# State-space loop of a decoder trunk: output tables summed on TensorE, input tables first, sine tables and one Toeplitz transfer moved

## Chip, cores and metric

The kernel runs on one core of one Trainium2 chip. The metric is the device time of one execution in microseconds (us). The kernel before has a median of 1282.83 us over 3 runs, from 1282.32 to 1284.73.

## What is computed

The reference is a decoder trunk for one sequence of 512 tokens with 16 learned tokens in front (528 in all) and width 1024. Its first layer is a state-space mixer (S5), the second is attention; each has a feed-forward part behind it. The change lies in the mixer:

```python
def s5_mixer(u, a_re, a_im, log_dt, b_re, b_im, c_re, c_im, d_skip, w_glu):
    ...
    bu_re = jnp.einsum('blgc,gpc->blgp', u32, bbar_re)
    bu_im = jnp.einsum('blgc,gpc->blgp', u32, bbar_im)
    ...
    _, _, x_re, x_im = lax.associative_scan(combine, (a_seq_re, a_seq_im, bu_re, bu_im), axis=1)
    y = (jnp.einsum('blgp,gcp->blgc', x_re, c_re.astype(f32))
         - jnp.einsum('blgp,gcp->blgc', x_im, c_im.astype(f32)))
    y = (y + d_skip.astype(f32).reshape(S5_GROUPS, S5_GROUP) * u32).reshape(bsz, L, D_MODEL)
    z = jax.nn.gelu(y)
    vg = jnp.einsum('bld,de->ble', z, w_glu.astype(f32))
    val, gate = jnp.split(vg, 2, axis=-1)
    return (val * jax.nn.sigmoid(gate)).astype(u.dtype)
```

There are 64 groups of 16 channels, with 64 complex states in each group. The state `x` obeys a linear recurrence over the tokens with a complex factor per state.

## The kernel before

**Chunks and octets.** The 528 tokens are cut into 66 chunks of 8 (`T = 8`, `NCH = 66`). What the tokens of a chunk do to one another is a Toeplitz matrix; what is carried from chunk to chunk is a state. The 64 groups are taken 8 at a time: octet 0 to octet 7 (`o`, `KD = 8`). For octet i the text uses these short names:

- **e(i)**, the input tables (`e_stage`, L244 to L268): one small product (L248), four wide ones on VectorE (L259 to L266), and two sums on GpSimd (L262, L267). Their tile `e` has one buffer, so e(i+1) waits until TensorE has transposed e(i) (`e_trans`, L274 to L279; ScalarE copies the result out at L282).
- **v(i)** (`v_mm`, L285 to L291): the octet's inputs times the transposed input tables. GpSimd first scales those inputs in place (**u(i)**, `u_stage`, L296) by `rsu`, a reciprocal root which VectorE works out in small steps (`rs_chain`, L456 to L476).
- **rot(i)** (`rot`, L584 to L614): eleven VectorE operations which turn v by cosine and sine tables (`ct`, `st`), scan over the chunks (L603) and turn back. They leave the states `s`.
- **o(i)**, the output tables (`o_stage`, L548 to L563): VectorE makes `ot` (L560) and `to` (L561), GpSimd adds `to` to `ot` (L562).
- **r(i)** (`r_mm`, L565 to L576): 8 TensorE products of `op` with `ot` (L571) and 4 narrow ones with the diagonal table `dg` (L573), in four quarters; each product fills 32 partitions of the PSUM bank `rp`. ScalarE copies the bank to `rsb` (L575).
- **m(i)** (`m_dma`, L578 to L582): `rsb` is written to DRAM (`rd`) and read back, with another stride, as the Toeplitz tiles `m`. Both transfers issue on SyncE (SP).
- **y(i)** (`y_mm`, L616 to L628): for each of 8 groups one product of the inputs with `m` (L624) and one of `s` with `ot` (L625), accumulated in PSUM. ScalarE copies the result to `ysb` (L627). `z_out` (L630) transposes it and takes the gelu, `z_low` (L643 to L644) makes its lower part on VectorE.

**Fill steps.** While the loop runs, TensorE already multiplies the finished parts of z by the GLU weights: `fill(n)` does n steps of the generator `glu1`, and the table `FILLS` (L35) says how many in each iteration. One step is one tile of 128 rows of z against one weight tile, six products of 264 columns. Its weight is loaded by SP (L98) and split in a high part on ScalarE (`wh`, L113) and a low part on VectorE (`wl`, L114).

**Order.** The order on each engine is the order in which the program's lines are written; there is no scheduler. Iteration i of the loop (L690 to L736) does, in this order: r(i); the copy of the small tile of e(i+1); y(i-1); m(i); loads; the transposes of e(i+1); rot(i) with z_low(i-2) inside; o(i+1); u(i+2) and e(i+2); a first lot of fill steps; z_out(i-1); v(i+1); a second lot of fill steps. The loads of residual inputs `h` from `xn` issue at L709, one in each iteration from the third on. Before the loop come the steps of the start: squares of the inputs on ScalarE with their sums on TensorE (`square`, `fold`; the first `SQB = 6` of the eight stand ahead of the cosine and sine of `sincos`, L400 to L402); phases by repeated addition on GpSimd (`int_powers`, L404 to L413, on the tile `phx` for the tables of octets 2 to 7); and the sine tables `tables(0)` (beside the output factors) and `tables(1)` to `tables(3)` (L688, L450 to L454 on ScalarE), each for two octets.

Of the kernel before, what the change touches and what calls it, by code (L numbers as in the profile page):

```python
# [23 lines left out]
T = 8  # L24
# [7 lines left out]
SQB = 6  # L32
# [3 lines left out]
N1F = len(GLU1)  # L36
PAIRS = (6, 0, 4, 1, 3, 2, 5, 7)
# [10 lines left out]
def trunk_kernel(ctx, tc, xu, xn, prm, octp, gvec, c_id, c_rev, c_i16, c_blk, c_mask,  # L48
# [148 lines left out]
    with ExitStack() as s5x:  # L197
# [112 lines left out]
        with tc.tile_pool(name="init", bufs=1) as ini:  # L310
# [93 lines left out]
            def int_powers(p, cnt):  # L404
                w = p.shape[2]
                n = 2
                while n < cnt:
# [10 lines left out]
            int_powers(ph, T + 1)  # L418

            pool.tensor_copy(phc[0][:, 1, :], ph[:, T, 0:8])  # L420
            int_powers(phc[0], NCH)
# [91 lines left out]
            def e_rs():  # L513
                yield from e_stage(0)
                pool.tensor_copy(phx[:, 1, :], ph[:, T, 8:NPAIR])
                int_powers(phx, NCH)
                e_fin(0)
                yield from rs_chain()
# [4 lines left out]
            v_mm(0)  # L523
            drain(e_stage(1))
# [13 lines left out]
        oc3 = s5x.enter_context(tc.tile_pool(name="oct3", bufs=3))  # L538
# [9 lines left out]
        def o_stage(o):  # L548
# [9 lines left out]
            ot = oc3.tile([128, 8, n, CH], F32, tag="ot", name="ot")  # L558
            to = oc.tile([128, 8, n, CH], F32, tag="to", name="to")
            dve.tensor_tensor(out=ot, in0=xb(0), in1=yb(y1), op=ALU.mult)  # L560
            dve.tensor_tensor(out=to, in0=xb(1), in1=yb(y2), op=ALU.mult)  # L561
            pool.tensor_tensor(out=ot, in0=ot, in1=to, op=ALU.add)  # L562
            oo[o] = ot  # L563

        def r_mm(o):  # L565
            ot, p = oo[o], opd.pop(o)
            bb = p[:, 448:704].rearrange("p (g c) -> p g c", g=8)
            rp = bank2("rp")[:, 0]
            for q in range(4):
                for g2 in range(2):  # L570
                    pe.matmul(rp[32 * q:32 * q + 32, 0:128], lhsT=bb[:, 2 * q + g2, :],  # L571
                              rhs=ot[:, 2 * q + g2, 0:T, :].rearrange("p s c -> p (s c)"), start=(g2 == 0), stop=False)
# [43 lines left out]
        def y_mm(o):  # L616
            u, ot, m, s = uu.pop(o), oo.pop(o), mtile[o % 2], stile[o % 2]
            yp = bank2("yp")
            ysb = oc.tile([NCH, T, 8, CH], F32, tag="ysb", name="ysb")
            for b in range(2):  # L620
                for g in range(4 * b, 4 * b + 4):
# [3 lines left out]
                    pe.matmul(yo, lhsT=s[:, q, g2, 0:NCH], rhs=ot[:, g, 1:, :].rearrange("p s c -> p (s c)"), start=False, stop=True)  # L625
# [62 lines left out]
        for j in range(1, 4):  # L688
            tables(j)
        for i in range(0, KD + 3):  # L690
# [5 lines left out]
            if ini_:  # L696
# [7 lines left out]
            if ini_:  # L704
# [3 lines left out]
            if 0 <= b - 1 < KD:  # L708
                sp.dma_start(out=h[b - 1], in_=xn[:, b - 1, :])  # L709
            if ina:  # L710
                e_trans(a)
                dec_stage(a)
            if ini_:
                rg = rot(i)
                next(rg)
                next(rg)
                if 0 <= b - 1 < KD:
                    z_low(b - 1)
                next(rg)
                drain(rg)  # L720
            elif 0 <= b - 1 < KD:
                z_low(b - 1)
            if ina:
                o_stage(a)
            if a + 1 < KD:
                u_stage(a + 1)
                drain(e_stage(a + 1))
            fill(fl[0])
# [598 lines left out]
```

## Time and profile before

| | |
|---|---|
| device time, median of 3 runs | 1282.83 us (1282.32 to 1284.73) |
| the profiled execution | 1283.81 us |
| its span in the trace | 1282.0 us |
| TensorE busy (PE) | 1207.2 us, 94% of the span |
| VectorE busy (DVE) | 707.8 us, 55% |
| ScalarE busy (ACT) | 484.6 us, 38% |
| GpSimd busy (POOL) | 326.4 us, 25% |
| TensorE by 40 equal slices of 32 us | `3588899999999999999999989999999999999996` |
| VectorE by the same slices | `8899547643433343433678888985644444442224` |
| granted TensorE clock by slice | `8689899999999999999999999999999999999998` |

A digit is the busy share of a slice in tenths, and 9 is 90% or more; in the last row it is the granted clock in tenths of full speed. The loop takes the first five or six slices. The profiled execution is one run of its own: its time and its span are what durations from the trace are added up against. A line number such as L571 is the line of the kernel's program, PE is the matrix engine's products, and a row of the time order gives its start in the span, its length, its engine, line, operation, result and sources, and in brackets the time that its engine stood idle ahead of it and what ended that.

### The profile page before, as it was taken

Reading aid. Unit: us, or ns where it says so; the run is one execution under the profiler, and the core shown is the slowest. Engines: PE = TensorE matmul, PEld = TensorE weight load, DVE = VectorE, ACT = ScalarE, POOL = GpSimd, SP = SyncE. Lnnn points to the kernel's source line nnn. Section 1 sums busy time; section 2 is a strip of 40 time slices with the busy share of each in tenths; the row PEclk is TensorE's granted clock in tenths of the full one; section 3 lists DMA queues with packets and bytes.
Section 4 is the critical chain, followed back from the end, with each engine's and each line's share of the span. In section 5 each row is a group of like instructions: output and inputs, shape, how many; then the busy total and the mean of one; then the engine's idle time right before and its main releaser. Section 6 shows DMA issues by size and latency. Waiting matters only on the chain.

```text
span 1282.0 us, 19763 instructions
## 1 busy us (share of the span) xinstructions
PE 1207.2 (94%) x8206; PEld 1100.9 (86%) x8206; DVE 707.8 (55%) x987; ACT 484.6 (38%) x738; POOL 326.4 (25%) x290
## 2 busy tenths in 40 slices
PE   3588899999999999999989999989999999999996
PEld 3578899999999999999979999868788888888886
DVE  8899547643433343433678888985644444442224
ACT  5544343432223222222557666753332323321120
POOL 6444027210110110111144444444311101111110
PEclk8689899999999999999999999999999999999998
DMA  3455523232233323333212221122233333223321
GB/s 98 88 110 114 106 77 110 77 117 86 83 100 86 94 81 91 91 91 95 87 50 57 62 64 50 50 66 80 69 99 99 99 99 94 88 88 96 102 74 66
DMA packets 44919, 110.15 MB, mean 86 GB/s; under 512 B 4766, under 2 KB 17950, under 8 KB 44830
## 3 DMA queue, kind: packets, MB, share of 16 engines
q1 hardware_dynamic: 43024, 107.64, 29.5%
q8 instruction: 64, 1.05, 0.3%
q10 hardware_dynamic: 1805, 1.26, 0.3%
q14 instruction: 26, 0.20, 0.1%
HBM read 106.14 MB, written 2.74 MB: 85 GB/s over the span
## 4 chain that ended last, share of the span: by engine, by line
PE 73%; DVE 6%; ACT 1%; issue 1%; POOL 0%; DVEq 0%; ACTq 0%; POOLq 0%
PE pgu L135 19%; PE po L135 18%; PE pu L135 10%; PE pg L135 10%; PE pj L135 7%; PE pj L1089 2%; DVE ga L985 2%; PE w L1027 1%; PE pv L1048 1%; PE po L1180 1%; DVE wl L114 1%; PE z L977 1%; PE z L1089 1%; PE z L976 1%; DVE xl L157 1%
## 5 line engine op out<-in xcount | busy, mean ns | idle before, releaser
L114 DVE TENSOR_TENSOR wl<-raw,wh 128x1024 fp32r<-128x1024 f32 (+5 forms) x194 | 242.8, 1257 | 223.8 <-ACT wh L113 220.4
L113 ACT ACTIVATE wh<-raw 128x1024 fp32r<-128x1024 f32 (+5 forms) x194 | 189.1, 979 | 242.4 <-PE po L135 120.2
L811 POOL TENSOR_TENSOR s<-s,rstd 128x528 f32<-128x528 f32 (+1 forms) x44 | 57.4, 1305 | 439.7 <-ACT s L810 439.7
L135 PE MATMUL pgu<-xl,wh 128*128 128x512 f32 x352 | 138.7, 394 | 1.0 <-DVE xl L157 1.0
L135 PE MATMUL pgu<-xh,wh 128*128 128x512 f32 x352 | 138.3, 393 | 0.6 <-ACT xh L156 0.6
L135 PE MATMUL pgu<-xh,wl 128*128 128x512 f32 x352 | 138.4, 393 | 0.0
L135 PE MATMUL po<-hh,wh 128*128 128x264 f32 (+1 forms) x506 | 132.0, 317 | 0.0
L135 PE MATMUL po<-hh,wl 128*128 128x264 f32 (+1 forms) x506 | 131.9, 317 | 0.0
L135 PE MATMUL po<-hl,wh 128*128 128x264 f32 (+1 forms) x506 | 131.8, 317 | 0.0
L135 PE MATMUL pg<-xh,wl 128*128 128x264 f32 x536 | 109.5, 286 | 2.3 <-DVE wl L114 2.3
L135 PE MATMUL pg<-xl,wh 128*128 128x264 f32 x536 | 109.6, 286 | 1.9 <-DVE xl L157 1.9
L135 PE MATMUL pg<-xh,wh 128*128 128x264 f32 x536 | 110.2, 287 | 1.2 <-ACT ysb L627 0.9
L998 POOL TENSOR_TENSOR be<-be,ga 128x415 f32<-128x415 f32 (+1 forms) x48 | 58.1, 1210 | 127.5 <-DVE ga L985 111.5
L135 PEld LDWEIGHTS po<-hh,wh 128*128 128x128 f32 x506 | 83.2, 188 | 7.2
L135 PEld LDWEIGHTS po<-hl,wh 128*128 128x128 f32 x506 | 83.3, 187 | 7.1
L135 PEld LDWEIGHTS po<-hh,wl 128*128 128x128 f32 x506 | 83.1, 188 | 7.1
L810 ACT ACTIVATE s<-g 128x528 f32<-128x528 f32 (+1 forms) x44 | 28.1, 638 | 153.9 <-DVE g L809 153.9
L135 PEld LDWEIGHTS pg<-xh,wl 128*128 128x128 f32 x536 | 83.3, 189 | 2.7 <-DVE wl L114 2.7
L135 PEld LDWEIGHTS pg<-xh,wh 128*128 128x128 f32 x536 | 83.5, 188 | 2.4 <-ACT ysb L627 1.6
L135 PEld LDWEIGHTS pg<-xl,wh 128*128 128x128 f32 x536 | 83.1, 188 | 2.6 <-DVE xl L157 2.6
L165 POOL TENSOR_TENSOR sq<-h 128x528 f32<-128x528 f32 (+1 forms) x27 | 36.8, 1363 | 173.2 <-DVE h L826 94.1
L135 PEld LDWEIGHTS pgu<-xl,wh 128*128 128x128 f32 x352 | 66.0, 188 | 17.0 <-DVE xl L157 1.7
(338 smaller groups left out, 2566.8 us busy)
## 6 DMA issues: line engine op xcount, KB each, us to landing
raw<-in_w_in SPq DMA_DIRECT2D x88, 512.0 KB, 3.5
raw<-in_w_out SPq DMA_DIRECT2D x32, 512.0 KB, 3.8
raw<-in_w_kv SPq DMA_DIRECT2D x16, 512.0 KB, 3.6
raw<-in_w_out SPq DMA_DIRECT2D x16, 384.0 KB, 3.2
m<-rd SPq DMA_DIRECT2D x8, 512.0 KB
raw<-in_w_q SPq DMA_DIRECT2D x8, 512.0 KB, 3.5
raw<-in_w_o SPq DMA_DIRECT2D x8, 512.0 KB, 3.4
op<-in_octp SPq DMA_DIRECT2D x8, 352.0 KB, 7.1
```

Source lines behind the costliest of these rows:

```text
L113: act.activation(out=wh[:, 0:nk, :], in_=r, func=ACTF.Copy)
L114: dve.tensor_tensor(out=wl[:, 0:nk, :], in0=r, in1=wh[:, 0:nk, :], op=ALU.subtract)
L135: pe.matmul(ps[pc][:, 0:n], lhsT=w[:, k, :], rhs=x[kk][:, c0:c0 + n], start=(first and k == 0 and j == 0), stop=(last and k == nk - 1 and ...
L157: dve.scalar_tensor_tensor(out=xl[k], in0=h[k][:, 0:n], scalar=g, in1=xh[k], op0=ALU.mult, op1=ALU.subtract)
L165: e.tensor_tensor(out=sq[:, 0:n], in0=h[k][:, 0:n], in1=h[k][:, 0:n], op=ALU.mult)
L810: act.activation(out=s_, in_=g_, func=ACTF.Silu)
L811: pool.tensor_tensor(out=s_, in0=s_, in1=rstd[:, 0:n], op=ALU.mult)
L976: pe.matmul(o_, lhsT=qhh[hd][:, q0:q0 + 128], rhs=khl[hd][:, k0:k0 + nn], start=True, stop=False)
L977: pe.matmul(o_, lhsT=ql[hd][:, q0:q0 + 128], rhs=khl[hd][:, k0:k0 + nn], start=False, stop=True)
L985: dve.tensor_tensor_scan(out=ga[:, c0:c1], data0=ga[:, c0:c1], data1=hide[:, m0:m0 + c1 - c0], initial=init, op0=ALU.mult, op1=ALU.max)
L998: pool.tensor_tensor(out=be[:, 1:n], in0=be[:, 1:n], in1=ga[:, 0:n - 1], op=ALU.mult)
L1089: pe.matmul(ps, lhsT=w[:, k, :], rhs=x[k], start=(k == 0 and j == 0), stop=(k == KD - 1 and j == 2))
```

## The change

- `o_stage` no longer adds the two output tables; `r_mm` and `y_mm` take both, one product each, into the same PSUM bank. Both tables now have two buffers (before: three of `ot`, one of `to`).
- In the loop, where there is an e(i+2), the order is now: z_low, first lot of fill steps, e(i+2), u(i+2), o(i+1). z_low stands behind rot(i) and no longer inside it.
- r(7) and m(7) move from the head of iteration 7 to the end of iteration 6, behind two of its second lot of five fill steps (`RAHEAD = 2`).
- `tables(1)` moves into iteration 0, behind the transposes; `tables(2)` and `tables(3)` to the head of iteration 1. Before, all three stood ahead of the loop.
- `SQB` is 5 instead of 6, and the two longest additions of `phx` move behind u(0) and v(0).
- The loads of the last three `h` issue after iteration 8 instead of one each in iterations 7 to 9.

```diff
--- before.py
+++ after.py
@@ -29,11 +29,12 @@
-SQB = 6
+SQB = 5
 PADW = (T - 1) * CH
 GLU1 = (2, 2, 2, 3, 3, 3, 4, 4, 5, 5, 5, 6, 7)
 FILLS = {3: (3, 3), 4: (5, 4), 5: (4, 4), 6: (5, 5), 7: (2, 3), 8: (2, 4), 9: (2, 5)}
 N1F = len(GLU1)
+RAHEAD = 2
@@ -401,10 +402,9 @@
...
-            def int_powers(p, cnt):
+            def int_steps(p, cnt, n=2, stop=1 << 10):
                 w = p.shape[2]
-                n = 2
-                while n < cnt:
+                while n < min(cnt, stop):
                     m = min(n, cnt - n)
                     pool.tensor_tensor(out=p[:, n, :], in0=p[:, n // 2, :], in1=p[:, n // 2, :], op=ALU.add)
                     if m > 1:
@@ -415,10 +415,10 @@
             for j in range(4):
                 square(j)
                 fold(j)
-            int_powers(ph, T + 1)
+            int_steps(ph, T + 1)
 
             pool.tensor_copy(phc[0][:, 1, :], ph[:, T, 0:8])
-            int_powers(phc[0], NCH)
+            int_steps(phc[0], NCH)
             for j in range(4, SQB):
                 square(j)
                 fold(j)
@@ -513,7 +513,7 @@
             def e_rs():
                 yield from e_stage(0)
                 pool.tensor_copy(phx[:, 1, :], ph[:, T, 8:NPAIR])
-                int_powers(phx, NCH)
+                int_steps(phx, NCH, 2, 16)
                 e_fin(0)
                 yield from rs_chain()
 
@@ -521,6 +521,7 @@
             e_trans(0)
             u_stage(0)
             v_mm(0)
+            int_steps(phx, NCH, 16)
             drain(e_stage(1))
             for c0, c1 in ((0, 4), (4, NPAIR)):
                 if c0:
@@ -535,7 +536,6 @@
 
         oc = s5x.enter_context(tc.tile_pool(name="oct", bufs=1))
         oc2 = s5x.enter_context(tc.tile_pool(name="oct2", bufs=2))
-        oc3 = s5x.enter_context(tc.tile_pool(name="oct3", bufs=3))
@@ -555,21 +555,21 @@
-            ot = oc3.tile([128, 8, n, CH], F32, tag="ot", name="ot")
-            to = oc.tile([128, 8, n, CH], F32, tag="to", name="to")
+            ot = oc2.tile([128, 8, n, CH], F32, tag="ot", name="ot")
+            to = oc2.tile([128, 8, n, CH], F32, tag="to", name="to")
             dve.tensor_tensor(out=ot, in0=xb(0), in1=yb(y1), op=ALU.mult)
             dve.tensor_tensor(out=to, in0=xb(1), in1=yb(y2), op=ALU.mult)
-            pool.tensor_tensor(out=ot, in0=ot, in1=to, op=ALU.add)
-            oo[o] = ot
+            oo[o] = (ot, to)
 
         def r_mm(o):
-            ot, p = oo[o], opd.pop(o)
+            tabs, p = oo[o], opd.pop(o)
             bb = p[:, 448:704].rearrange("p (g c) -> p g c", g=8)
             rp = bank2("rp")[:, 0]
             for q in range(4):
                 for g2 in range(2):
-                    pe.matmul(rp[32 * q:32 * q + 32, 0:128], lhsT=bb[:, 2 * q + g2, :],
-                              rhs=ot[:, 2 * q + g2, 0:T, :].rearrange("p s c -> p (s c)"), start=(g2 == 0), stop=False)
+                    for j, tab in enumerate(tabs):
+                        pe.matmul(rp[32 * q:32 * q + 32, 0:128], lhsT=bb[:, 2 * q + g2, :],
+                                  rhs=tab[:, 2 * q + g2, 0:T, :].rearrange("p s c -> p (s c)"), start=(g2 == 0 and j == 0), stop=False)
                 pe.matmul(rp[32 * q:32 * q + 32, 0:CH], lhsT=ident[:, 32 * q:32 * q + 32], rhs=dg[:, o, :], start=False, stop=True)
             rsb = oc.tile([128, T * CH], F32, tag="rsb", name="rsb")
             act.activation(out=rsb, in_=rp[:, 0:128], func=ACTF.Copy, scale=gv[:, G_MIX0, o:o + 1])
@@ -614,7 +614,7 @@
                 dve.tensor_tensor(out=s[64:128, :, g2, 1:], in0=t1[a, 1], in1=t2[a, 0], op=ALU.add)
 
         def y_mm(o):
-            u, ot, m, s = uu.pop(o), oo.pop(o), mtile[o % 2], stile[o % 2]
+            u, tabs, m, s = uu.pop(o), oo.pop(o), mtile[o % 2], stile[o % 2]
             yp = bank2("yp")
             ysb = oc.tile([NCH, T, 8, CH], F32, tag="ysb", name="ysb")
             for b in range(2):
@@ -622,7 +622,8 @@
                     q, g2 = divmod(g, 2)
                     yo = yp[0:NCH, b, 128 * (g % 4):128 * (g % 4) + 128]
                     pe.matmul(yo, lhsT=u[:, g, :], rhs=m[:, g, :], start=True, stop=False)
-                    pe.matmul(yo, lhsT=s[:, q, g2, 0:NCH], rhs=ot[:, g, 1:, :].rearrange("p s c -> p (s c)"), start=False, stop=True)
+                    for j, tab in enumerate(tabs):
+                        pe.matmul(yo, lhsT=s[:, q, g2, 0:NCH], rhs=tab[:, g, 1:, :].rearrange("p s c -> p (s c)"), start=False, stop=(j == 1))
             for b in range(2):
                 act.activation(out=ysb.rearrange("p t (b g) c -> p b g t c", b=2)[:, b], in_=yp[0:NCH, b].rearrange("p (g t c) -> p g t c", g=4, t=T), func=ACTF.Copy)
             ysbs[o] = ysb
@@ -685,15 +686,16 @@
         o_stage(0)
         sc_stage(1)
         loads(2)
-        for j in range(1, 4):
-            tables(j)
         for i in range(0, KD + 3):
             a, b = i + 1, i - 1
             fl = FILLS.get(i, (0, 0))
             ina, inb, ini_ = 0 <= a < KD, 0 <= b < KD, 0 <= i < KD
             if i == 1:
                 w_load(AHEAD)
-            if ini_:
+                tables(2)
+                tables(3)
+            own = i < KD - 1
+            if own:
                 rsb = r_mm(i)
             if ina:
                 e_fin(a)
@@ -701,38 +703,45 @@
                     sc_stage(a)
             if inb:
                 y_mm(b)
-            if ini_:
+            if own:
                 m_dma(i, rsb)
             if a + 2 < KD:
                 loads(a + 2)
-            if 0 <= b - 1 < KD:
+            if 0 <= b - 1 < KD - 3:
                 sp.dma_start(out=h[b - 1], in_=xn[:, b - 1, :])
             if ina:
                 e_trans(a)
                 dec_stage(a)
+                if i == 0:
+                    tables(1)
             if ini_:
-                rg = rot(i)
-                next(rg)
-                next(rg)
-                if 0 <= b - 1 < KD:
-                    z_low(b - 1)
-                next(rg)
-                drain(rg)
-            elif 0 <= b - 1 < KD:
+                drain(rot(i))
+            if 0 <= b - 1 < KD:
                 z_low(b - 1)
-            if ina:
+            if a + 1 < KD:
+                fill(fl[0])
+                drain(e_stage(a + 1))
+                u_stage(a + 1)
                 o_stage(a)
-            if a + 1 < KD:
-                u_stage(a + 1)
-                drain(e_stage(a + 1))
-            fill(fl[0])
+            else:
+                if ina:
+                    o_stage(a)
+                fill(fl[0])
             if inb:
                 z_out(b)
             if ina:
                 v_mm(a)
-            fill(fl[1])
+            if a == KD - 1:
+                fill(RAHEAD)
+                m_dma(a, r_mm(a))
+                fill(fl[1] - RAHEAD)
+            else:
+                fill(fl[1])
             if i == 2:
                 w_split(AHEAD)
+            if i == KD:
+                for k in range(KD - 3, KD):
+                    sp.dma_start(out=h[k], in_=xn[:, k, :])
         fill(1000)
 
         ssq = new_ssq(NTOK)
```

How the change moves instructions, at three places. Names as above; `raw` is a weight tile as loaded, `xl` the low part of z, `sb` the small product of e, `t` a tile of rot.

VectorE, from the output tables of one iteration of the middle to the next rot; in the kernel before it is iteration 5:

```order
L560 TENSOR_TENSOR ot<-sc,y_105 128x1152
L561 TENSOR_TENSOR to<-sc,y_106 128x1152
L248 TENSOR_TENSOR sb<-op 128x128
L259 TENSOR_TENSOR e<-sb,pr 128x4x112
L261 TENSOR_TENSOR ta<-sb,pr 128x448
L264 TENSOR_TENSOR e<-sb,pr 128x4x112
L266 TENSOR_TENSOR tb<-sb,pr 128x448
L114 TENSOR_TENSOR wl_1274<-raw_1098,wh_1273 128x640
L114 TENSOR_TENSOR wl_1337<-raw_1155,wh_1336 128x640
L595 TENSOR_TENSOR t_1420<-vp,ct 128x528
```

And the same stretch of the changed kernel, from the end of rot(5):

```order
L645 TENSOR_TENSOR xl_430<-zf,xh_422 128x528
L115 TENSOR_TENSOR wl_1336<-raw_1145,wh_1335 128x640
L249 TENSOR_TENSOR sb<-op 128x128
L260 TENSOR_TENSOR e<-sb,pr 128x4x112
L262 TENSOR_TENSOR ta<-sb,pr 128x448
L265 TENSOR_TENSOR e<-sb,pr 128x4x112
L267 TENSOR_TENSOR tb<-sb,pr 128x448
L560 TENSOR_TENSOR ot<-sc,y_105 128x1152
L561 TENSOR_TENSOR to<-sc,y_106 128x1152
L115 TENSOR_TENSOR wl_1415<-raw_1218,wh_1414 128x640
L595 TENSOR_TENSOR t_1514<-vp,ct 128x528
```

The output tables moved from the head of the stretch to its end, and a weight split (the low part of a fill step's weight) now stands ahead of the input tables.

GpSimd at the start, from the third-longest phase addition to the sums of e(1); before:

```order
L411 TENSOR_TENSOR phx<-phx 128x168
L409 TENSOR_TENSOR phx<-phx 128x24
L411 TENSOR_TENSOR phx<-phx 128x360
L409 TENSOR_TENSOR phx<-phx 128x24
L411 TENSOR_TENSOR phx<-phx 128x744
L409 TENSOR_TENSOR phx<-phx 128x24
L411 TENSOR_TENSOR phx<-phx 128x24
L296 TENSOR_TENSOR h_77<-h_77,rsu 128x528
L262 TENSOR_TENSOR e<-e,ta 128x4x112
```

And now:

```order
L411 TENSOR_TENSOR phx<-phx 128x168
L297 TENSOR_TENSOR h_77<-h_77,rsu 128x528
L409 TENSOR_TENSOR phx<-phx 128x24
L411 TENSOR_TENSOR phx<-phx 128x360
L409 TENSOR_TENSOR phx<-phx 128x24
L411 TENSOR_TENSOR phx<-phx 128x744
L409 TENSOR_TENSOR phx<-phx 128x24
L411 TENSOR_TENSOR phx<-phx 128x24
L263 TENSOR_TENSOR e<-e,ta 128x4x112
```

The scaling u(0) moved ahead of the six last phase additions, which now stand between it and the sums of e(1).

SP's queue at the end of the loop, from the load of a fill weight of 896 columns on; before (`L580` and `L582` are m(7)):

```order
L98 DMA raw_1444<-in_w_glu 128x896
L98 DMA raw_1512<-in_w_glu 128x128
L580 DMA rd_417<-rsb 8x16x128
L582 DMA m_411<-rd_417 128x8x128
L709 DMA h_82<-in_xn 128x528
L98 DMA raw_1606<-in_w_glu 128x1024
L709 DMA h_83<-in_xn 128x528
L98 DMA raw_1680<-in_w_glu 128x768
L709 DMA h_84<-in_xn 128x528
```

And now:

```order
L99 DMA raw_1537<-in_w_glu 128x896
L99 DMA raw_1605<-in_w_glu 128x128
L580 DMA rd_414<-rsb 8x16x128
L582 DMA m_408<-rd_414 128x8x128
L99 DMA raw_1714<-in_w_glu 128x1024
L99 DMA raw_1795<-in_w_glu 128x768
L744 DMA h_82<-in_xn 128x528
L744 DMA h_83<-in_xn 128x528
L744 DMA h_84<-in_xn 128x528
```

The two transfers of m(7) keep their place among the weight loads, though r(7) ahead of them moved on TensorE; the three loads of `h` moved behind the weight loads.

## Rows read from the trace of the kernel before

**Rows 1.** Waits of TensorE, 20 to 240 us: for what; us in all, times, longest.

```profile
PE yp L624 <- DMA m<-rd: 9.7, 3, 4.9
PE rp L571 <- POOL ot L562: 9.6, 3, 4.9
PE yp L624 <- ACT rsb L575: 0.5, 1, 0.5
```

**Rows 2.** Time order of VectorE, 99 to 116 us: start, length, line, operation, tiles.

```profile
99.57 1.36 DVE L560 TENSOR_TENSOR ot<-sc,y 128x1152 f32<-128x1152 f32 x1
102.11 0.29 DVE L248 TENSOR_TENSOR sb<-op 128x128 f32<-128x128 f32 x1
104.67 3.84 DVE L114 TENSOR_TENSOR wl<-raw,wh 128x384 fp32r<-128x384 f32 x3
108.43 0.69 DVE L595 TENSOR_TENSOR t<-vp,ct 128x528 f32<-128x528 f32 x1
115.57 1.36 DVE L560 TENSOR_TENSOR ot<-sc,y 128x1152 f32<-128x1152 f32 x1
```

**Rows 3.** Stretches by window (length, busy time per engine, clock), then time order of TensorE.

```profile
89.97:164.64 74.67, 64.72 (x645) 62.34 (x646) 54.59 (x81) 30.96 (x63) 21.56 (x12) 0.95 0.51 111
...
140.44:143.91 3.47, 3.47 (x36) 3.47 (x33) 3.39 (x7) 0.37 (x1) 0.00 (x0) 1.00 0.07 19
153.27:159.62 6.35, 6.35 (x32) 6.35 (x33) 0.00 (x0) 0.00 (x0) 0.00 (x0) 0.53 0.22 89
...
139.10 0.65 PE L571 MATMUL rp<-ot,op 128*32 128x128 f32 x6
...
139.59 0.41 PE L571 MATMUL rp<-ot,op 128*32 128x128 f32 x4
139.84 0.41 PE L571 MATMUL rp<-ot,op 128*32 128x128 f32 x4
...
140.44 0.43 PE L624 MATMUL yp<-m,h 128*66 128x128 f32 x2
...
153.27 0.66 PE L624 MATMUL yp<-m,h 128*66 128x128 f32 x2 [4.89 <-DMA m<-rd]
```

**Rows 4.** A stretch by window; time order of GpSimd and VectorE, 31 to 35 us.

```profile
27.86:31.79 3.93, 1.76 (x32) 1.56 (x30) 3.93 (x5) 2.42 (x7) 3.93 (x8) 0.50 0.00 0
...
31.79 2.65 POOL L562 TENSOR_TENSOR ot<-ot,to 128x1152 f32<-128x1152 f32 x1
...
32.55 2.17 DVE L598 TENSOR_TENSOR t<-t,t 128x264 f32<-128x264 f32 x1
```

**Rows 5.** Time order of TensorE, then of ScalarE, after y(3).

```profile
95.39 1.04 PE L279 MATMUL ep<-ident,e 128*128 128x128 f32 x8
...
97.83 0.53 ACT L113 ACTIVATE wh<-raw 128x384 fp32r<-128x384 f32 x1
```

**Rows 6.** Time order, 31 to 60 us, of ScalarE, of TensorE, of VectorE.

```profile
31.73 0.64 ACT L452 ACTIVATE pha<-phx 128x528 f32<-128x528 int32 x1
...
41.33 0.35 ACT L575 ACTIVATE rsb<-rp,gv 128x128 f32<-128x128 f32 x1
...
53.02 0.66 PE L624 MATMUL yp<-m,h 128*66 128x128 f32 x2 [4.06 <-DMA m<-rd]
...
58.40 1.04 PE L279 MATMUL ep<-ident,e 128*128 128x128 f32 x8
...
59.53 0.62 DVE L259 TENSOR_TENSOR e<-sb,pr 128x448 f32<-128x448 f32 x1 [3.49 <-PE ep L279]
```

**Rows 7.** Time order of VectorE, 12 to 27 us.

```profile
12.37 0.50 DVE L445 TENSOR_TENSOR pr<-mg,cs 128x288 f32<-128x288 f32 x1 [1.53 <-ACT cs L402]
...
22.90 1.72 DVE L475 SCALAR_TENSOR_TENSOR rsu<-tt,rsu 128x66 f32<-128x66 f32 x1
...
26.11 0.29 DVE L248 TENSOR_TENSOR sb<-op 128x128 f32<-128x128 f32 x1
```

**Rows 8.** A stretch by window: TensorE idle in a fill step, 103 to 106 us.

```profile
103.64:105.39 1.75, 0.00 (x1) 0.01 (x1) 1.75 (x5) 0.34 (x1) 1.75 (x2) 1.00 0.22 80
```

## The prediction

> **What bounds the kernel now.** The profile's first part has TensorE busy for 94% of the span, so I first asked where it is not: in the table of equal slices TensorE is fed without a gap from about 165 us on, and the change touches nothing that runs later except loads. Whatever it does must show as a shift of that point. I take as the mark the start of the last seven fill steps, 164.64 us in the trace; what follows is a chain of matmuls that moves with it.
>
> Ahead of the mark I read three views. The list of waits says for whom TensorE stood still: for m, the Toeplitz matrix read back from DRAM, and for GpSimd's sum of the two output tables [rows 1]. The time order of VectorE says what set the pace: from one o(i) to the next 16.0 us without an idle mark [rows 2]. Of these o takes 2.54, e 2.56, three weight splits 3.76 and rot with z_low 7.14. So the loop is VectorE's in the middle, and TensorE has slack. The third view is the end of the loop: the last y waits 4.89 us for m(7), then runs at half clock: 6.35 us against 3.47 for y(6) [rows 3].
>
> **What the change does to each part, and what it costs.**
>
> *The sum on GpSimd goes.* It takes 2.65 us [rows 4], eight times, and r stands behind it. In its place TensorE gets eight more products in each r and eight in each y. For y the price is clear: 16 products take 3.47 us at full clock [rows 3], so 24 take 5.21, plus 1.74. For r no row has the new form. Now 12 products take 1.34 us [rows 3]; by their number, 8 more are 0.9. The bounds: a quarter of r starts 0.25 us after the one before though its four wide passes last 0.41 [rows 3]; if only the starting of six passes counts (0.04 each), 16 more passes are 0.67; if nothing of the added work overlaps, at y's rate, 1.74, or 2.1 with the present overlap lost too. I take 0.9, since the program form is the nearest. At half clock all of this doubles.
>
> Here a rule can be weighed. The rows show quarters overlapping, 0.25 against 0.41. The Trainium skill (TensorEngine Tiling (Array Packing), Key Properties) says that tiles operate independently and different tiles run in parallel; the added products go to the same tile as their neighbours, so by the rule alone nothing says they overlap. By it r could grow by 2.1 instead of 0.9; that is a rival below.
>
> *Input tables ahead of output tables, first fill ahead of both.* VectorE now runs rot, z_low, the split of fill 1, e, o, the split of fill 2. The split needs ScalarE's wh, which stands behind the copy of y(i-1): from the end of y to the start of wh are 2.44 us [rows 5], and wh takes 0.53. So a new circle closes: r, y, 2.97, split 0.5 (as wh), e, o, next r. With 2.24 for r, 5.21, 5.1 for e and o and 0.2 for hand-over it is 16.25 us for r(3) to r(4). VectorE, with 7.14 for rot and z_low, would be through sooner and now waits some 3 us. In iterations without fills (1 and 2) e waits for e_trans, which follows y: 1.13 us after y's end [rows 6], then 2.1 of e (2.56 less some 0.4 for its first step, which doesn't wait), 2.54 of o and 0.2, so r to r is 2.24 + 5.21 + 1.13 + 4.8 = 13.4.
>
> *Phase steps and first squares at the start.* VectorE waits 1.53 us for the cosine [rows 7]; with one square fewer ahead of it ScalarE could deliver while it now sits idle. The next thing needed is the first load of octp, whose landing I can't see: 0 to 1.5, I take 0.7. One step of the reciprocal root takes 1.72 us [rows 7] beside GpSimd's long phase steps, while the six steps behind it take 0.25 each: 1.5 saved by putting those behind u_stage(0). e(1) starts at 26.11 - 2.2 = 23.9 instead.
>
> *First m.* o(0) is then done at 29.0, r(0) takes 2 x 2.24 = 4.5 at half clock, and GpSimd's diagonal table now queues behind the moved phase steps (0 to 2, I take 0.5): the copy rsb(0) at 34.0. Now it starts at 41.33, because three sine tables stand ahead of it from 31.73 on [rows 6]. The lead is 7.3, and m(0) lands at 53.02 - 7.3 = 45.7. The tables are 3.2 each; two of them now stand ahead of rsb(1), which is done by about 48. m(1) follows by 11.7 (41.33 to 53.02), at 59.7, and y(1) could start at 59.6: just covered. If the cover fails, each us is paid.
>
> One more place for a rule. rot(0) will run beside what GpSimd does from 27.86 on, e(1), the diagonal table and u(1). In the rows, one step of it took 2.17 us and ended within 0.3 of the sum's end [rows 4]; I let rot(0) grow by 2.2 in all, which stays hidden. The Trainium skill (SBUF — State Buffer, SBUF: two separate sides) says that the shared port pair is an exclusive lock and the loser fully blocks for the whole instruction. All of these, 3.9 us [rows 4], could then stand in rot(0)'s way, and r(1) and y(0) would start 1.7 later than I have it; the trace agrees for that one step, and no row shows the alternation.
>
> *From there to r(4).* y(0) at 45.7, 5.7 long with a short rest of half clock; 1.13, 2.1, 2.54, 0.2: r(2) at 57.4. Then 13.4: r(3) at 70.8. Then 16.25: r(4) at 87.05, against 89.97 now, **2.9 us earlier**.
>
> *From r(4) to the mark* TensorE is the bound in the changed kernel. The stretch is 74.67 us now, 64.72 busy [rows 3]. Take off 2.88, the half clock of y(7); add 4 x 0.9 for r(4) to r(7) and 5 x 1.74 for y(3) to y(7): 74.1 of work. Waits that stay: y(3), y(4) and y(5) behind the copy of r, which the list of waits has once at 0.5 [rows 1] and which the order of PSUM use now makes three: 1.5. m(7) leaves after r(7), which is moved ahead of three fill steps; from the start of r(7) to y(7) are now 14.2 us [rows 3], so some 15 with the longer r, against 14.1 of work between: 1.0. Small ones 0.5. Together 77.1, **2.4 us later**. The last three loads of h now issue after the loop; the first use is a sum on GpSimd more than 10 us behind, so I cost them at nothing; if they came late, they would hold that sum and not TensorE's next matmul. The loads for weights keep their place.
>
> The sum is -2.9 + 2.4 = **-0.5 us**: 1283.3 for the profiled execution of 1283.81, whose span is 1282.0. The median of the runs is 1282.83, 1.0 below that execution, so I forecast 1282.3.
>
> **The rivals.**
>
> *Faster, the lead is kept.* The same circle with the low ends: r plus 0.67 instead of 0.9 on seven r (1.6), no wait behind the copy (1.5), clock up at y(0) (0.5), m(7) landing 1.0 sooner. 4.6 more, so 1277.7. For it: these are all inside what the rows allow. Against it: each is a separate favour.
>
> *Slower, the added products of r don't overlap.* Place: r(2) to r(7), all in the circle or in the bound stretch. Price: 2.1 instead of 0.9, six times 1.2, so +7.2: 1289.5. It decides from about 0.5 us above my price on. For it: the same tile is used twice as long before the next one starts. Against it: the overlap that the rows show now is large.
>
> *Slower, the clock falls.* Before r(2) and r(3) TensorE idles about 2.4 us in the new order. The 4.89 us before y(7) brought the half clock, 1.2 instead of 2.4 GHz, and cost 2.9 [rows 3]; 1.75 us without a product, from 103.64 on, did not, the granted clock stayed at 1.00 [rows 8]. 2.4 lies between, nearer to the shorter. One fall makes 1285.2, two 1288. The same price comes if m(7) stays as late as now.
>
> *The change does not do what it says* would be an m(7) that still ends last by several us; it is in the last case.
>
> **How the numbers follow.** A measurement of this kernel can tell about 0.2%, 2.6 us, from no change. The forecast has a chance of 0.42, with its own range 1280 to 1285, all inside that bound; the faster rival 0.31; no overlap 0.11; the falling clock 0.16. So faster 0.31, same 0.42, slower 0.27. The range reaches to 1276.5, a little past the faster rival, and to 1288 for two falls; outside it lie the no-overlap case and about 0.07 of the faster one.
>
> **What would show it.** Right: r(4) starts near 87, VectorE waits about 3 us for wh in each iteration from 3 on, TensorE's busy time grows by about 20 us (8 x 2.6), the m(7) wait is near 1 instead of 4.89, r is near 2.2. Wrong: an r of 3.4, half clock after r(2) or r(3), a mark more than 3 us from 164, or time that changes after the mark.

## The result, and the profile after

The change makes the kernel slower: a median of 1290.81 us over 4 runs (1290.61 to 1293.01) against 1282.57 us for the kernel before, beside which it ran. The ratio is 1.0068 with a 95% interval from 1.0055 to 1.008. The forecast was 1282.3 with a range up to 1288.0, so the range missed it. The case that came nearest was the one I had given 0.11: the added products of r don't overlap.

In the page of the changed kernel TensorE is busy 25.4 us longer (1232.6 against 1207.2), where I had 20.8:

```profile
span 1288.7 us, 20283 instructions
...
PE 1232.6 (96%) x8462; PEld 1124.6 (87%) x8462; DVE 698.3 (54%) x987; ACT 484.4 (38%) x738; POOL 301.5 (23%) x282
```

The windows of the changed kernel show r(2), r(3), r(7), y(7) and the stretch from r(4) to the mark. The columns are those of [rows 3]: start and end, length, busy time and number of instructions of TensorE, of its weight loads, of VectorE, ScalarE and GpSimd, then the granted clock, the DMA share and GB/s.

```profile
58.24:62.71 4.47, 4.47 (x39) 3.88 (x39) 4.40 (x8) 0.00 (x0) 0.00 (x0) 0.62 0.01 2
73.93:76.81 2.88, 2.88 (x39) 2.85 (x39) 2.85 (x7) 0.00 (x0) 0.00 (x0) 1.00 0.58 184
145.46:148.55 3.09, 3.09 (x40) 3.06 (x40) 3.06 (x7) 0.00 (x0) 0.00 (x0) 1.00 0.00 0
160.33:165.49 5.16, 5.16 (x50) 5.16 (x49) 0.71 (x1) 0.17 (x1) 0.00 (x0) 1.00 0.54 184
89.56:170.50 80.94, 77.35 (x788) 74.94 (x789) 50.07 (x81) 30.87 (x63) 8.10 (x8) 1.00 0.43 100
```

r(7) takes 3.09 us with TensorE busy throughout; it took 1.34 [rows 3]. That is 1.75 more where I had put 0.9. y(7) takes 5.16 at full clock, close to the 5.21 of the forecast. r(2) took 4.47; its granted clock of 0.62 is the mean of a stretch that began at 1.2 and ended at 2.4 GHz. A window of r runs to the start of the next product; the expectations below count to the end of r's last product and so have 1.42 and 3.16 where the windows have 1.34 and 3.09.

TensorE's time order in the changed kernel, first at r(2) to r(4), then at the mark:

```profile
57.02 0.38 PE L571 MATMUL rp<-ot,op 128*32 128x128 f32 x2 [1.58 <-issue]
58.24 0.61 PE L571 MATMUL rp<-to,op 128*32 128x128 f32 x2 [0.84 <-DVE to L561]
...
72.72 0.38 PE L571 MATMUL rp<-ot,op 128*32 128x128 f32 x2 [1.59 <-issue]
73.93 0.41 PE L571 MATMUL rp<-to,op 128*32 128x128 f32 x2 [0.84 <-DVE to L561]
...
89.56 0.38 PE L571 MATMUL rp<-ot,op 128*32 128x128 f32 x2 [0.27 <-issue]
90.77 0.41 PE L571 MATMUL rp<-to,op 128*32 128x128 f32 x2 [0.84 <-DVE to L561]
...
170.50 0.41 PE L136 MATMUL pg<-xh,wh 128*128 128x264 f32 x2
```

r now begins with its first product with `ot` and then waits 0.84 us for `to`. Counted from the second product, r(4) starts at 90.77, 0.8 later than before, where the forecast had it 2.9 earlier. The mark lies at 170.50 against 164.64, 5.9 later. Behind the mark little changed: 1288.7 - 170.5 = 1118.2 us, before 1282.0 - 164.64 = 1117.4.

### The profile page after: what moved, and what is told of

It is laid out like the page before. It is cut to its first block, busy times and chain, and to the rows that moved or that the text cites. A ratio compares the mean times of both kernels' runs of the same rounds, so it can differ in the third digit from the quotient of the medians.

```text
span 1288.7 us, 20283 instructions
## 1 busy us (share of the span) xinstructions
PE 1232.6 (96%) x8462; PEld 1124.6 (87%) x8462; DVE 698.3 (54%) x987; ACT 484.4 (38%) x738; POOL 301.5 (23%) x282
## 4 chain that ended last, share of the span: by engine, by line
PE 73%; DVE 6%; ACT 1%; issue 1%; POOL 0%; DVEq 0%; ACTq 0%; POOLq 0%
PE pgu L136 19%; PE po L136 18%; PE pu L136 10%; PE pg L136 10%; PE pj L136 7%; PE pj L1098 2%; DVE ga L994 1%; PE w L1036 1%; PE pv L1057 1%; PE po L1189 1%; DVE wl L115 1%; PE z L986 1%; PE z L1098 1%; PE z L985 1%; DVE xl L158 1%
## 5 line engine op out<-in xcount | busy, mean ns | idle before, releaser
L115 DVE TENSOR_TENSOR wl<-raw,wh 128x1024 fp32r<-128x1024 f32 (+5 forms) x194 | 236.5, 1224 | 236.8 <-ACT wh L114 233.4
L136 PEld LDWEIGHTS pgu<-xh,wh 128*128 128x128 f32 x352 | 66.0, 188 | 16.4 <-ACT xh L157 1.1
```

Of the source, the lines that this page charges most:

```text
L115: dve.tensor_tensor(out=wl[:, 0:nk, :], in0=r, in1=wh[:, 0:nk, :], op=ALU.subtract)
L136: pe.matmul(ps[pc][:, 0:n], lhsT=w[:, k, :], rhs=x[kk][:, c0:c0 + n], start=(first and k == 0 and j == 0), stop=(last and k == nk - 1 and ...
```

## The experiments

I had two theories of r's growth. *Theory A*: products for the same quarter of the array (the same 32 partitions of the bank) wait for one another, products for different quarters overlap. In the program one quarter's four products now stand in a row. *Theory B*: each product costs its own time in any order. A third, *theory C*, blamed the new order of e, fill and o for the loss.

**All four quarters in turn.** The loops of r are exchanged, and the four narrow products come last:

```diff
-            for q in range(4):
-                for g2 in range(2):
-                    for j, tab in enumerate(tabs):
+            for j, tab in enumerate(tabs):
+                for g2 in range(2):
+                    for q in range(4):
...
+            for q in range(4):
                 pe.matmul(rp[32 * q:32 * q + 32, 0:CH], lhsT=ident[:, 32 * q:32 * q + 32], rhs=dg[:, o, :], start=False, stop=True)
```

> Edit: the changed kernel with r's products in another order: all four quarters of the array take one product each, then all four the next (quarter innermost), instead of four products in a row on one quarter. Work and operands are the same. Theory A (a product waits for the one before it on the same quarter, products on different quarters overlap; so each added product in a row costs its full 0.22 us, and r grew from 1.42 to 3.16): r falls to about 1.0 to 1.4 us, some 1.9 less for each of r(2) to r(7), and the time by 8 to 12 us, to 1279 to 1283. Theory B (each product of r costs about 0.17 us for its weights, in whatever order): r stays at 3.1 and the time at 1290 to 1291.

Measured: 1279.08 us (1277.44 to 1280.83), ratio to the kernel before 0.9965 [0.9953, 0.9977]; 11.7 us less than the change by the medians. r(7) of this kernel in the windows, and its y(1), y(3), y(5) and mark in TensorE's time order:

```profile
135.75:136.81 1.06, 1.06 (x41) 1.03 (x41) 1.06 (x3) 0.00 (x0) 0.00 (x0) 1.00 0.00 0
```

```profile
59.80 0.43 PE L625 MATMUL yp<-m,h 128*66 128x128 f32 x2
...
88.41 0.43 PE L625 MATMUL yp<-m,h 128*66 128x128 f32 x2 [0.53 <-ACT rsb L576]
...
121.53 0.43 PE L625 MATMUL yp<-m,h 128*66 128x128 f32 x2 [0.51 <-ACT rsb L576]
...
158.75 0.41 PE L136 MATMUL pg<-xh,wh 128*128 128x264 f32 x2
```

The same three of the changed kernel:

```profile
62.71 0.43 PE L624 MATMUL yp<-m,h 128*66 128x128 f32 x2
...
94.18 0.43 PE L624 MATMUL yp<-m,h 128*66 128x128 f32 x2 [0.46 <-ACT rsb L575]
...
131.26 0.43 PE L624 MATMUL yp<-m,h 128*66 128x128 f32 x2 [0.46 <-ACT rsb L575]
```

r(7) falls from 3.09 to 1.06 with the same products, and the distance grows from place to place: 2.9 us at y(1), 5.8 at y(3), 9.7 at y(5), 11.75 at the mark. Theory B falls, and with a cheap r the new order of the loop loses nothing, which speaks against theory C too. The order of r's products alone decides the sign of the whole change. Products for the same quarter have both its part of the array and its 32 partitions of the bank in common; which of these makes them wait, these runs don't separate.

**GpSimd's sum put back into the change.**

```diff
-            oo[o] = (ot, to)
+            pool.tensor_tensor(out=ot, in0=ot, in1=to, op=ALU.add)
+            oo[o] = (ot,)
...
```

> Edit: the changed kernel with GpSimd's sum of the two output tables put back, so that r and y take one table as before; all else of the change stays. Theory A (the two tables on TensorE are what costs: 1.74 in each r and in each y of the bound stretch): TensorE's busy time falls by some 26 us, r is 1.4 and y 3.5 again, r waits some 2 us for the sum where TensorE runs dry, and the time is 1276 to 1281. Theory C (the new order, input tables behind the first fill step's split, is what costs): 1287 or more, since the circle stays and the sum of 2.65 us comes back into it.

Measured: 1294.11 us (1292.89 to 1295.44), ratio 1.0083 [1.0067, 1.0099]. My expectation by theory A was wrong, and the number by theory C, 1287 or more, came. TensorE's busy time fell by 22.6 us, to 1210.0, but its list of waits begins so:

```profile
PE rp L572 <- POOL ot L562: 34.9, 7, 8.8
PE vp L292 <- POOL h L297: 6.7, 1, 6.7
```

In the new order the output tables come last before r, and a sum behind them stands bare in front of seven r's. So the new order costs waits where the sum stands in it; with two tables and a cheap r the kernel with all four quarters in turn shows no such loss. The change's order needs the two tables; the parts can't be priced apart and added.

**The two tables alone, in the order of before.** The same edits to `o_stage`, `r_mm` and `y_mm` as in the change, two buffers each, and nothing else.

> Edit: the kernel before with the two tables on TensorE alone (two buffers each); order, sine tables, start and r(7) as before. Theory A: the sum's 2.65 us is gone where VectorE sets the pace, but from the point at which TensorE is the bound r and y cost 1.74 more each, so 1285 to 1290, with the wait for m(7) still there at 3 to 5 us. Theory C: about 1280, because the loop of before had slack on TensorE.

Measured: 1290.81 us (1289.37 to 1293.48), ratio 1.006 [1.0044, 1.0077], just above the range by theory A; theory C's 1280 did not come. The loss is there without the new order.

**r(7) and m(7) alone, in the kernel before.** They leave the head of iteration 7 and stand at the end of iteration 6:

```diff
-            if ini_:
+            own = i < KD - 1
+            if own:
                 rsb = r_mm(i)
...
-            fill(fl[1])
+            if a == KD - 1:
+                fill(2)
+                m_dma(a, r_mm(a))
+                fill(fl[1] - 2)
+            else:
+                fill(fl[1])
```

> Edit: the kernel before with r(7) and m(7) alone moved to the end of iteration 6, behind two fill steps. If the wait for m(7) and the half clock behind it were worth what the rows say, 4.89 + 2.88, the time falls by 6 to 8 us, to 1275 to 1277. Rival: what stood in the way there was hidden by other work, or comes back as a wait for the weights: less than 3 us, 1280 or more.

Measured: 1278.35 us (1276.99 to 1280.55), ratio 0.9962 [0.9949, 0.9976]: 4.9 us less by the medians, between my two cases; the mark moved from 164.64 to 158.38:

```profile
158.38 0.41 PE L135 MATMUL pg<-xh,wh 128*128 128x264 f32 x2
```

This is as much as the whole change with r's quarters in turn brings (0.9965): beyond this one step, the rest of the change together brings nothing that shows.

**Quarters in turn in the kernel before.** The same exchange of loops, with one table.

> Edit: the kernel before with r's products in quarter-innermost order (one table, GpSimd's sum, everything else as before). By theory A (products wait on the same quarter only) r falls from 1.42 to about 0.65 us; that counts only where TensorE is the bound, for r(5) to r(7), so the time falls by 0 to 2.5 us, 1280 to 1283. By theory B (each product costs by itself) r stays at 1.4.

Measured: 1282.78 us (1280.44 to 1286.46), ratio 1.0003 [0.9994, 1.0011]. r(7) took 0.62 us instead of 1.34, as theory A says; the time did not move. TensorE waits for the sum instead, 11.8 us in its list of waits, where it was 9.6 [rows 1]:

```profile
PE rp L571 <- POOL ot L562: 11.8, 3, 4.9
```

r's order counts where r is in the chain, and in the kernel before it is not. There is also less to win there, 0.72 us in each r against 2.03.

**Both of these together.**

> Edit: the kernel before with r(7) and m(7) moved as in the change, and r's products quarter-innermost; GpSimd's sum, order and start as before. If the two gains are independent: 1278.4 less 0 to 2.5, 1275.5 to 1278.5. If the shorter r only lets TensorE wait longer for VectorE: 1278.

Measured: 1278.3 us (1277.33 to 1280.7), ratio 0.9965 [0.9952, 0.9977], the same as with r(7) moved alone.

**The old order in the changed kernel**, r's quarters in turn, once with the sum on GpSimd and once with two tables:

```diff
-            if a + 1 < KD:
-                fill(fl[0])
-                drain(e_stage(a + 1))
-                u_stage(a + 1)
-                o_stage(a)
...
+            if ina:
+                o_stage(a)
+            if a + 1 < KD:
+                u_stage(a + 1)
+                drain(e_stage(a + 1))
+            fill(fl[0])
```

> Edit: the changed kernel with three things different: GpSimd's sum back, the order of before in the loop (output tables, then input tables, then the first fill steps), r's products quarter-innermost. So the start, the sine tables and r(7) are the change's. If the earlier start (e(1) 3.3 us earlier, the first y 6 us earlier) carries through a loop that VectorE bounds: 3 us below the previous kernel of this call, 1272 to 1275. If the lead is lost at the sum or at the half clock: 1276 to 1279.

> Edit: the changed kernel with the order of before in the loop (output tables, then input tables, then the first fill steps) and r's products quarter-innermost; two tables on TensorE, start, sine tables and r(7) as in the change. If the changed order (input tables and a split first) is what holds the lead back: 3 to 5 us below the change with quarters alone, which was 1279.1, so 1274 to 1276. If the order helps, as its waits for the copy-free r say: 1280 or more.

Measured: with the sum 1279.15 us (1277.76 to 1279.65), ratio 0.9966 [0.9952, 0.9979]; with two tables 1279.95 (1278.3 to 1283.02), ratio 0.9979 [0.997, 0.9988]. The first of them has all of the change but the order and the two tables, and it is no faster than the kernel before with r(7) moved and quarters in turn (0.9966 against 0.9965): the earlier start does not carry through. The second, beside the change with all four quarters in turn (0.9965), differs in the order alone: with two tables and a cheap r the order of e and o makes no difference that these runs can tell. With the sum it seems to: 1294.11 in the new order against 1279.15 in the old, though r's order differs between these two as well.

**Two quarters in turn.** r takes quarters 0 and 1 in turn, then 2 and 3.

> Edit: the changed kernel with r's products going over two quarters in turn, first quarters 0 and 1, then 2 and 3 (the narrow products with the diagonal last). Theory A, in numbers: the products of one quarter follow one another every 0.22 us and each pair of quarters has four such steps, so r takes 2 x 4 x 0.22 = 1.75 plus some 0.1, against 3.16 with one quarter at a time and 1.2 with all four in turn; 1.3 to 1.4 less for six r's, so 8 us less than the change: 1282 to 1284. Theory B' (only a change of the quarter between neighbours matters, not how many quarters are in turn): as with all four, 1279.

Measured: 1279.52 us (1278.32 to 1281.79), ratio 0.9977 [0.9968, 0.9986]. One r, at full clock, in the windows of this kernel:

```profile
103.11:104.70 1.59, 1.59 (x41) 1.49 (x40) 1.59 (x4) 0.00 (x0) 0.18 (x1) 1.00 0.00 0
```

r takes 1.59 us, less than the 1.85 of theory A's steps, and the time is the one of all four in turn, as theory B' has it; r itself is not (1.59 against 1.06). That a neighbour in the queue goes to another quarter is worth 1.50 us of each r (3.09 to 1.59); four instead of two give another 0.53, which the time does not show. Why it doesn't stays open. One thing that took some of it back in the profiled executions is the clock: with all four quarters in turn it fell at r(3), with two in turn it was 1.00 there. This is r(3) of the kernel with four:

```profile
70.20:72.51 2.31, 1.85 (x41) 1.35 (x41) 2.31 (x5) 0.08 (x1) 1.15 (x1) 0.58 0.31 113
```

**Only r(0) to r(3) in turn.**

> Edit: the changed kernel with r's products over all four quarters in turn for r(0) to r(3) only; r(4) to r(7) as in the change. If the first half of the loop is a circle through r, as forecast, its saving passes on in full: in the kernel with all r's in turn y(2) starts 4.3 us earlier than in the change, so 1286 to 1287. If VectorE sets the pace there, the saving is lost in a wait for the output tables: 1289 to 1291.

Measured: 1285.61 us (1282.83 to 1287.09), ratio 1.0016 [1.0007, 1.0024]; the mark is at 165.10, 5.4 us ahead of the change's:

```profile
165.10 0.41 PE L136 MATMUL pg<-xh,wh 128*128 128x264 f32 x2
```

The saving of the first half passes on, as it should if the circle through r that I forecast for it is there.

**The sum on GpSimd behind r, for y alone.** r takes both tables, quarters in turn; then GpSimd adds them, and y takes the sum. With the order of the change, and with the order of before:

```diff
...
                 pe.matmul(rp[32 * q:32 * q + 32, 0:CH], lhsT=ident[:, 32 * q:32 * q + 32], rhs=dg[:, o, :], start=False, stop=True)
+            pool.tensor_tensor(out=tabs[0], in0=tabs[0], in1=tabs[1], op=ALU.add)
...
-                    for j, tab in enumerate(tabs):
+                    for tab in tabs[:1]:
...
```

> Edit: the changed kernel with r's products over all four quarters in turn, and with GpSimd's sum of the two tables back, but issued behind r and used by y alone (r takes the two tables, y the sum). The 1.75 us that each y costs more is saved without a wait for the sum in front of r: five times in the stretch that TensorE bounds, and in the circle twice: 1269 to 1273. Rival: GpSimd's 2.65 us hold VectorE's steps up beside it (2.17 instead of 0.4 in the kernel before) or the sums of e behind them, and half or more is lost: 1274 to 1279.

> Edit: the same with the order of before in the loop (output tables, input tables, fill steps). The order made no difference of more than 1 us with y on two tables (1279.1 and 1280.0); with a shorter y VectorE becomes the bound of the loop again, as in the kernel before: 1272 to 1276. If the saving in y counts in full: 1270.

Measured: in the order of the change 1275.6 us (1273.51 to 1280.28), ratio 0.9943 [0.9929, 0.9957], the lowest median of all, though its interval meets that of r(7) moved alone; in the order of before 1286.51 (1286.17 to 1287.78), ratio 1.0026 [1.0015, 1.0037]. The first fell into the range of its rival, 1274 to 1279; the second is 10 us above what I expected. VectorE's and GpSimd's time order of the second kernel, in one iteration:

```profile
95.74 2.62 POOL L575 TENSOR_TENSOR ot<-ot,to 128x1152 f32<-128x1152 f32 x1 [1.26 <-PE rp L571]
98.33 1.39 POOL L297 TENSOR_TENSOR h<-h,rsu 128x528 f32<-128x528 f32 x1
...
96.16 2.49 DVE L600 TENSOR_TENSOR t<-t,t 128x264 f32<-128x264 f32 x1
98.58 1.44 DVE L601 TENSOR_TENSOR t<-t,t 128x264 f32<-128x264 f32 x1
99.94 1.29 DVE L605 TENSOR_TENSOR_SCAN w<-dec,t 128x264 f32<-128x264 f32 x2
```

The first of these steps in the changed kernel, where GpSimd is idle at that time:

```profile
42.85 0.43 DVE L598 TENSOR_TENSOR t<-t,t 128x264 f32<-128x264 f32 x1
```

The two small steps of rot end 0.3 us behind GpSimd's two operations: the sum and u hold VectorE up by 3.1 us in this iteration (2.49 + 1.44 against twice 0.43). In the order of before the output tables stand right behind rot and z_low, so r(i+1) comes later by as much. In the order of the change rot(4) is held up as well, by 2.3 us (2.70 and 0.42 against twice 0.43):

```profile
90.70 2.62 POOL L575 TENSOR_TENSOR ot<-ot,to 128x1152 f32<-128x1152 f32 x1 [1.51 <-PE rp L571]
90.91 2.70 DVE L600 TENSOR_TENSOR t<-t,t 128x264 f32<-128x264 f32 x1
...
93.53 0.42 DVE L601 TENSOR_TENSOR t<-t,t 128x264 f32<-128x264 f32 x1
...
98.97 0.55 DVE L115 TENSOR_TENSOR wl<-raw,wh 128x384 fp32r<-128x384 f32 x1
```

But there the split of a weight stands between rot and the output tables. At this split VectorE stood idle for 4.15 us in the changed kernel, and here it does not:

```profile
102.47 0.56 DVE L115 TENSOR_TENSOR wl<-raw,wh 128x384 fp32r<-128x384 f32 x1 [4.15 <-ACT wh L114]
```

Two things take the place of that wait: the delay of rot itself, 2.3, and wh, which with the shorter r and y is done 8.6 us after the start of rot(4), where it was 11.3. That this is the whole difference between the two orders is argued; it was not tried by itself.

## Why the prediction was wrong

**The step that failed is r's price**: "12 products take 1.34 us [rows 3]; by their number, 8 more are 0.9". The mean counted the four narrow products with the wide ones, and it hid where the overlap was. In the trace of before each quarter had two wide products, and the second overlapped the first of the next quarter: 0.25 us from quarter to quarter [rows 3]. Now each has four, and only the last overlaps with the next quarter. Two quarters of r(7) in the changed kernel:

```profile
145.70 0.38 PE L571 MATMUL rp<-to,op 128*32 128x128 f32 x2
145.92 0.38 PE L571 MATMUL rp<-ot,op 128*32 128x128 f32 x2
146.14 0.27 PE L571 MATMUL rp<-to,op 128*32 128x128 f32 x1
146.15 0.30 PE L571 MATMUL rp<-ot,op 128*32 128x128 f32 x1
...
146.36 0.21 PE L573 MATMUL rp<-dg,ident 128*32 128x16 f32 x2
146.39 0.38 PE L571 MATMUL rp<-to,op 128*32 128x128 f32 x2
```

At 146.14 the last `to` of one quarter and the first `ot` of the next start together; the two products ahead of them start 0.22 apart, with no other quarter beside them. From quarter to quarter there are now 0.69 us (145.70 to 146.39), three times 0.22 and a little, as 0.25 was once 0.22 and a little. Eight added products at 0.22 are 1.75, the price of y's, and that is what r(7) grew by. Read so, the rows of before held the right price; I took an average over a row of products whose overlap lay at the seams.

This can be counted. Let products for one quarter start 0.22 us apart, let those for quarters in turn start together, and let one step overlap at each seam. Then r has 16 - 3 = 13 steps in the changed kernel, 8 - 1 = 7 with two quarters in turn and 4 with four; with one table it has 8 - 3 = 5, and 2 in turn. That is an estimate from the rows above: 2.86, 1.54, 0.88, 1.10 and 0.44 us, against 3.09, 1.59, 1.06, 1.34 and 0.62 measured. The measured times are 0.05 to 0.24 longer; they have the four narrow products in them.

The Trainium skill (TensorEngine Tiling (Array Packing), Key Properties) says that tiles operate independently and that different tiles can load weights and multiply in parallel. The runs agree, with 3.09, 1.59 and 1.06 us for one, two and four quarters in turn. I had quoted it for the right case, that neighbours on the same tile need not overlap, and then took the average all the same.

Point by point, by the steps of the forecast:

- *y plus 1.74.* Right: 94.18 to 99.47 is 5.29 for y(3), and y(7) took 5.16.
- *The start.* e(1) came at 22.77 (forecast 23.9), y(0) at 47.05 (forecast 45.7; before 53.02). r(0) waited 1.2 us for the diagonal table and y(0) 1.1 for m(0).
- *r(4) 2.9 us earlier.* Wrong: 0.8 later. Of the 3.7 between, y(0) had 1.35; r(2) to r(3) took 15.7 instead of 13.4, with r's price and the half clock of r(2) in it; r(3) to r(4) took 16.8 instead of 16.25; y(0) to r(2) gave 0.5 back.
- *r(4) to the mark 2.4 later.* 5.1 later by 90.77 to 170.50 against 74.67. Four r's at up to 0.85 above my price are some 3.3 more (r(4) had its first product done ahead of its window); m(7) cost no wait at all where I had 1.0, and y(7) ran at full clock.
- *VectorE waits some 3 us for wh from r(3) on.* Right: 3.08 and 4.15 in the next two iterations.
- *The clock.* The rival's fall came once. Ahead of r(2) TensorE stood idle 1.58 and 0.84 us, and r(2) ran at 0.62; ahead of r(3) it stood idle 1.59 and 0.84 and kept 1.00. So r(2) took 4.47 and not 2.88, 1.6 more.
- *GpSimd beside rot.* That rot grows beside GpSimd I had seen in one row [rows 4] but called hidden; in the last pair of runs it stands, with 3.1 us in an iteration, where VectorE sets the pace, and the time is 10.9 us longer; that the one makes the other is argued above.

r's price is the largest of the misses but not the only one. The measured mark lies 6.4 us behind the forecast one. Of this r(2) to r(7) at 0.64 to 0.85 above my price are about 4.5, the half clock of r(2) is 1.6 and the late y(0) 1.35; m(7) and the way from y(0) to r(2) gave 1.5 back. (Most of the rest of the 8.5 us by medians: 0.8 behind the mark, and the profiled execution of before, 1.0 above its median, had me take 1.0 off.) With r alone put right the forecast would have been near 1287, inside the range. That the no-overlap case's 1289.5 came so near 1290.81 is part luck: it had r 0.35 too dear, and the clock and y(0) made up for it.

The range should have held the no-overlap case: my own bound for r, 2.1, was in the text, gave 1289.5, and the rows at the seams spoke for it. The 0.11 was the mistake, not the list of cases.

What is left open: why the first half of the change (start, sine tables) brings no time once r is cheap. The earlier y(0) is in the traces, and in the old order with GpSimd's sum the lead is gone by r(4), which starts at 93.33 against 89.97; with two tables r(4) is still 4 us earlier (85.97 with all four quarters in turn, against 89.97) and the lead is gone at the mark, where y's price is the likely reason. I did not try each of them alone.

## What to carry to other kernels

Price added matmuls by their neighbours in the queue, not by an average: look in the time order which products start together and which in a row, and where a product goes to its own part of the array, let neighbours go to different parts. That reordering adds no work and was worth 11.7 us here, while in a kernel whose chain didn't run through these products it was worth nothing. A sum moved from one engine to another is priced with the order around it: the same sum cost 34.9 us of waits in one place, held VectorE in a second, and behind its first user it gave the lowest median of all.

## What the runs showed of the hardware

Sixteen products of 128 columns into 32 partitions each, with four narrow ones, took 3.09 us with four in a row on a quarter, 1.59 with two quarters in turn and 1.06 with four, at a granted clock of 1.00.

A step of VectorE with both sources from SBUF tiles ended 0.3 us behind the operation of GpSimd beside it, 2.49 us for a step of 0.43. In the same kernel the wide products of e, which take the small table from a PSUM bank, showed nothing of it, 0.61 us beside GpSimd's 1.15:

```profile
109.30 1.15 POOL L263 TENSOR_TENSOR e<-e,ta 128x448 f32<-128x448 f32 x1 [9.58 <-DVE ta L262]
...
109.58 0.61 DVE L267 TENSOR_TENSOR tb<-sb,pr 128x448 f32<-128x448 f32 x1
```

The Trainium skill (SBUF — State Buffer, SBUF: two separate sides) calls the shared port pair an exclusive lock against a GpSimd operation for a VectorE one with two SBUF inputs; the rows agree.

Behind the same idle time of 2.4 us the granted clock was 0.62 over r(2) of the changed kernel and 1.00 over its r(3). In the kernel with all four quarters in turn it was 1.00 over r(2), behind 1.58 us without a product, and 0.58 over r(3), behind 1.98. What decides it these runs don't show.
